# Sparse attention stage of a twelve-stage kernel: zero-padded keys, rotary terms read from PSUM, another order of its first projections

## The chip, the cores and the metric

The kernel runs on one core of a Trainium2 chip. Its engines are named as the profile names them: PE multiplies matrices (PEld is its weight load), DVE is the vector engine, ACT the scalar engine with its tables of functions, POOL the general engine, and SP issues the DMAs. The metric is the device time of one execution in microseconds (us); lower is better.

## The reference, cut to what matters

The program is two transformer blocks of depth 2, on 256 tokens of width 1024 in float32. The change is in the mixer of the first block's second layer, a sparse attention: 8 index heads score the keys, the 64 best causal keys of each query are kept, and 16 heads of 64 channels attend to these alone. Queries have 16 heads, while keys, values and index keys have one head that all share.

```python
q, k, v, qi, ki, wi = split_cols(h @ w_in, SA_SPLITS)        # 1024, 64, 64, 512, 64, 8 columns
q = apply_rope(rms_norm(q.reshape(b, L, ATT_HEADS, ATT_HEAD_DIM), q_norm), cos, sin)
k = apply_rope(rms_norm(k, k_norm)[:, :, None, :], cos, sin)[:, :, 0]
qi = apply_rope(qi.reshape(b, L, IDX_HEADS, IDX_DIM), cos, sin)
ki = apply_rope(ki[:, :, None, :], cos, sin)[:, :, 0]
...
logits = jnp.einsum('bthd,bsd->btsh', qib, ki).astype(jnp.float32)
score = jnp.einsum('btsh,bth->bts', jax.nn.relu(logits), wib.astype(jnp.float32)) * idx_scale
score = jnp.where(causal[None], score, -jnp.inf)
_, sel = lax.top_k(score, topk)                                # topk = 64
...
s = jnp.einsum('bthd,btkd->bthk', qb, k_sel).astype(jnp.float32) * att_scale
s = jnp.where(valid[:, :, None, :], s, -jnp.inf)
p = jax.nn.softmax(s, axis=-1).astype(v_sel.dtype)
return jnp.einsum('bthk,btkd->bthd', p, v_sel)                 # then @ w_out, added to x
```

## The kernel before, in words

Twelve stages follow one another: for each layer a feed-forward, a mixer and a feed-forward. The residual stays in two tiles of 128 tokens (`X[0]`, `X[1]`, the token tiles t0 and t1). Every large product is made of float32 split in two parts: `mm3` (L170 to L174) multiplies high by high (L172), low by high (L173) and high by low (L174) into one PSUM bank. Weights are made ready by `prep` (L105): SP fetches a unit into one of four `raw` tiles, ACT rounds it to the high part `wh` (L133) and DVE takes the difference as the low part `wl` (L137). For a few units `on_pool` (L142) puts the difference on POOL: those of the second half of the query projection and rows 3, 5 and 6 of the output projection `sa_w_out`. PSUM's eight banks are `pj` (3, projections), `pa` (3) and `pb` (2).

The order of the instructions on each engine isn't written out. A scheduler of the framework, which simulates the engines at build time, chooses it under priorities (`urgent` raises one) and pins (`after`: this comes behind that instruction). An engine works through its own list in order, so a late instruction holds up all behind it.

The sparse stage `sparse` (L896 to L1123) begins at about 788 us of the span. In the feed-forward before it the tables of the rotary terms (`rope_tables`) and rows 0 to 2 of `sa_w_out` are made ready. Then come, in program order:

- the projection of keys, values, index keys and index weights (200 columns, evacuated by `ev_kv`) and of the index queries (512 columns, `ev_qi`), each for both token tiles together (`proj_nat` goes through the k tiles and within one through both token tiles, then evacuates t0 and t1);
- `rope` (L904): on a copy of the projection in SBUF (ACT, L936, L955, L1012), POOL multiplies by the sine (`rt`, L907), DVE by the cosine (L908) and adds both (L909); PE transposes the result (`transp`, L918) and ACT copies it to SBUF (L920);
- `select(t)` (L971 to L1000): index scores of a pair of heads per bank (L980), where a head's product is 64 rows deep and lies in the upper or the lower half of the partitions; a ReLU on ACT (L983), the weighted sum of 8 heads on DVE (L987, L989), then eight rounds of `max` and `match_replace` (L995, L996) and the mask `mb[t]` (L997 to L1000);
- `proj_q(0)` and `proj_q(1)`, the queries of heads 0 to 7 and 8 to 15; the norm `qr` of each head goes into the scale of the exponential (L1019, L1021 on DVE, L1023 on POOL);
- the attention: `scores` fills a bank with four heads (t0, 128 keys) or two (t1, 256 keys), per head one product of depth 64 (L1043) and one that adds the mask (L1045, the mask as the moving operand of a unit matrix `idb`); DVE takes the maximum (L1048) and scales it (L1049); ACT takes the exponentials (L1052); `values` transposes them (L1059), copies them (L1063, L1065) and multiplies by `v` (L1070); `close` divides by the sums;
- the output projection, t0 and then t1 (from 908.32 us on), and the addition to `X` (L1110).

ACT holds one set of function tables at a time. `ex` (L962) is an exponential of a zero, pinned behind `ev_qi`'s copy, so that the load of the exponential's table comes there.

## Time and profile before

| what | value |
|---|---|
| time, median of 3 runs | 2453.47 us (2443.68, 2453.47, 2455.34) |
| span of the profiled execution, first to last instruction | 2446.0 us |
| PE busy | 2414.0 us, 99% |
| DVE, ACT, POOL busy | 1480.9, 1212.3, 183.1 us (61%, 50%, 7%) |
| granted clock of PE, mean | 0.987 |
| sparse stage up to its output projection | about 788 to 908 us |

The profiled execution has no time listed beside its span, and the time around the span isn't shown; the three runs lie from 2.3 us below the span to 9.3 us above it. Busy time is that of instructions that ran, so a PE at half clock counts as busy. The granted clock (PEclk) is a share of full speed, 1.00 for 2.4 GHz and 0.50 for 1.2 GHz. An idle time in brackets stands before the instruction that ended it, with what it waited for.

### The profile page before, as it was taken

How to read it: one execution, taken by the hardware profiler on the slowest of the kernel's cores; microseconds unless marked ns; L12 is line 12 of the kernel's file. 1: busy time of each engine (PE TensorE's matmuls, PEld its weight loads, DVE VectorE, ACT ScalarE, POOL GpSimd, SP SyncE). 2: the span in 40 equal slices, each digit the busy share in tenths (PEclk: the TensorE clock that was granted, in tenths of full speed). 3: DMA queues.
4: the chain of work that ended last, by engine and by line, in shares of the span. 5: the costliest groups of instructions: out<-in, count | busy, mean ns of one | idle time of the engine just before them, and what ended most of it. 6: DMA issues, size and time to landing. Idle time of an engine off the chain costs nothing.

```text
span 2446.0 us, 31525 instructions
## 1 busy us (share of the span) xinstructions
PE 2414.0 (99%) x11588; PEld 1979.5 (81%) x11588; DVE 1480.9 (61%) x2086; ACT 1212.3 (50%) x1868; POOL 183.1 (7%) x189
## 2 busy tenths in 40 slices
PE   8999999999999899999999999999999999999999
PEld 6888988888887678888888877888888887778887
DVE  5556786556555745556556685565565567756554
ACT  5445555445454435444445564454454455534543
POOL 0000330000000410000001020200000011101000
PEclk9999999999999879999999999999999999999999
DMA  7666545665665315655666543565566665335654
GB/s 237 192 193 181 146 126 177 199 186 177 205 214 159 114 35 163 189 186 189 189 188 188 163 129 110 171 209 188 181 198 189 190 184 160 117 104 172 202 186 136
DMA packets 301259, 417.15 MB, mean 171 GB/s; under 512 B 29168, under 2 KB 227248, under 8 KB 301104
## 3 DMA queue, kind: packets, MB, share of 16 engines
q1 hardware_dynamic: 300960, 414.66, 55.2%
q8 instruction: 91, 1.49, 0.3%
q14 instruction: 64, 0.52, 0.1%
q10 hardware_dynamic: 144, 0.48, 0.0%
HBM read 414.01 MB, written 1.05 MB: 170 GB/s over the span
## 4 chain that ended last, share of the span: by engine, by line
PE 95%; DVE 2%; issue 1%; DMA 1%; ACT 1%; POOL 0%; SPq 0%; DVEq 0%; POOLq 0%; ACTq 0%
PE pb L173 13%; PE pb L172 13%; PE pb L174 13%; PE pj L173 13%; PE pj L172 13%; PE pj L174 13%; PE pa L185 3%; PE pa L172 2%; PE pa L173 2%; PE pa L174 2%; PE pa L1043 1%; PE pa L809 1%; PE pa L1182 1%; DVE wl L137 1%; PE pb L1070 1%
## 5 line engine op out<-in xcount | busy, mean ns | idle before, releaser
L137 DVE TENSOR_TENSOR wl<-raw,wh 128x1024 fp32r<-128x1024 f32 x713 | 880.8, 1241 | 552.7 <-ACT wh L133 548.3
L133 ACT ACTIVATE wh<-raw 128x1024 fp32r<-128x1024 f32 (+1 forms) x720 | 755.5, 1054 | 579.2 <-PE pb L174 322.8
L172 PE MATMUL pb<-wh,qh 128*128 128x512 f32 x1408 | 551.6, 392 | 2.3 <-ACT qh L188 1.5
L173 PE MATMUL pb<-wl,qh 128*128 128x512 f32 x1408 | 550.1, 391 | 0.5 <-DVE wl L137 0.5
L174 PE MATMUL pb<-wh,ql 128*128 128x512 f32 x1408 | 549.8, 391 | 0.0
L172 PEld LDWEIGHTS pb<-wh,qh 128*128 128x128 f32 x1408 | 264.7, 188 | 58.3 <-ACT qh L188 1.8
L173 PEld LDWEIGHTS pb<-wl,qh 128*128 128x128 f32 x1408 | 264.8, 188 | 55.9 <-DVE wl L137 1.0
L174 PEld LDWEIGHTS pb<-wh,ql 128*128 128x128 f32 x1408 | 264.7, 188 | 55.6
L172 PE MATMUL pj<-wh,qh 128*128 128x512 f32 (+2 forms) x758 | 300.3, 399 | 1.9 <-ACT qh L188 1.7
L173 PE MATMUL pj<-wl,qh 128*128 128x512 f32 (+2 forms) x758 | 298.4, 394 | 1.3 <-DVE wl L137 1.3
L174 PE MATMUL pj<-wh,ql 128*128 128x512 f32 (+2 forms) x758 | 296.8, 395 | 0.3 <-DVE ql L189 0.3
L174 PE MATMUL pj<-wh,gl 128*128 128x512 f32 x432 | 173.8, 402 | 0.0
L172 PEld LDWEIGHTS pj<-wh,qh 128*128 128x128 f32 x758 | 143.7, 190 | 33.5 <-issue 3.9
L174 PEld LDWEIGHTS pj<-wh,ql 128*128 128x128 f32 x758 | 143.9, 190 | 32.2 <-issue 2.6
L173 PEld LDWEIGHTS pj<-wl,qh 128*128 128x128 f32 x758 | 144.0, 190 | 31.4 <-issue 2.9
L173 PE MATMUL pj<-wl,gh 128*128 128x512 f32 x432 | 168.5, 390 | 0.0
L172 PE MATMUL pj<-wh,gh 128*128 128x512 f32 x432 | 168.2, 391 | 0.0
L428 ACT ACTIVATE sg<-pb,nr 128x256 f32<-128x256 f32 x176 | 83.4, 474 | 148.3 <-PE pb L174 148.1
L430 DVE SCALAR_TENSOR_TENSOR g<-pb,nr,sg 128x256 f32<-128x256 f32 x176 | 84.6, 481 | 93.0 <-ACT sg L428 92.7
L188 ACT ACTIVATE gh<-pa 128x256 fp32r<-128x256 f32 x176 | 67.2, 382 | 130.9 <-PE pa L185 130.9
L257 POOL TENSOR_TENSOR nr<-nm,mhalf 128x1 f32<-128x1 f32 x24 | 14.2, 594 | 1471.9 <-DVE nm L255 1471.9
L189 DVE TENSOR_TENSOR gl<-pa,gh 128x256 fp32r<-128x256 f32 x176 | 74.4, 423 | 71.5 <-ACT gh L188 64.1
(522 smaller groups left out, 2908.2 us busy)
## 6 DMA issues: line engine op xcount, KB each, us to landing
raw<-in_ffn_w SPq DMA_DIRECT2D x352, 256.0 KB, 3.1
raw<-in_w_in SPq DMA_DIRECT2D x104, 512.0 KB, 4.0
raw<-in_ffn_w_gate SPq DMA_DIRECT2D x176, 256.0 KB, 2.9
raw<-in_ffn_w_up SPq DMA_DIRECT2D x176, 256.0 KB, 3.2
raw<-in_ffn_w_down SPq DMA_DIRECT2D x88, 512.0 KB, 3.6
raw<-in_ffn_w SPq DMA_DIRECT2D x88, 512.0 KB, 3.6
raw<-in_hy_w_in SPq DMA_DIRECT2D x44, 512.0 KB, 3.7
raw<-in_hy_w_out SPq DMA_DIRECT2D x16, 512.0 KB, 3.6
```

What stands on the lines that cost most here:

```text
L133: nc.scalar.activation(h[:, :n], r[:, :n], AF.Copy)
L137: eng.tensor_tensor(l[:, :n], r[:, :n], h[:, :n].bitcast(F32), op=OP.subtract)
L172: mm(out, a[0], b[0], start=start, stop=False)
L173: mm(out, a[0], b[1], start=False, stop=False)
L174: return mm(out, a[1], b[0], start=False, stop=stop)
L185: pe = nc.tensor.transpose(p[:, k * 128:(k + 1) * 128], src[:, k * 128:(k + 1) * 128], self.ident)
L188: act = nc.scalar.activation(hv, pv, AF.Copy)
L189: dve = nc.vector.tensor_tensor(lv, pv, hv.bitcast(F32), op=OP.subtract)
L428: nc.scalar.activation(sg, q[t][:, :256], AF.Silu, scale=rs[t])
L430: nc.vector.scalar_tensor_tensor(g, q[t][:, 256:], rs[t], sg, op0=OP.mult, op1=OP.mult)
L809: at["V", k] = nc.tensor.matmul(acc[t][:, h * dv:h * dv + dv], PT[:, j * 2 + b, :], vals(b, h), start=b == 0, stop=b == 1)
L1043: nc.tensor.matmul(S[:, j * nk:j * nk + nk].rearrange("p (t n) -> p t n", n=128), qT[b, t, g * 4 + h // 2, :], kkT[b, 0:t + 1, 1, :], star ...
```

## The change

- **Zero-padded keys.** The transposed keys lie in `kz` twice, once in the upper 64 partitions and once in the lower ones, with zeros in the other half. A product of depth 128 with the stacked queries of two heads then gives both heads' scores: 512 columns in one at t1, twice 256 at t0. This holds for the index scores and the attention's scores. `kz` is filled by two ACT copies of 64 partitions per tile and kind.
- **One mask product per bank.** The mask is the stationary or moving operand once for the 512 columns of a bank (`maskid` is -2^100 on the diagonal) and comes before the scores. The mask itself is one DVE instruction instead of two or three; the causal bias goes into the first step of the weighted sum (`cz`).
- **Rotary terms from PSUM.** `rope` reads the projection's bank and multiplies in place, all three instructions on DVE. The copy on ACT and POOL's product go away, and the bank is held until the third instruction. ACT's ReLU is in place in PSUM, and DVE's weighted sum reads PSUM.
- **Token tiles in turn.** `first_proj` multiplies keys and values of t0, index queries of t0, then both of t1, each evacuated at once.
- **First weights.** The first three units of `sa_w_in`, not rows 0 to 2 of `sa_w_out`, are made ready in the feed-forward before. Those rows' fetches and splits come in the sparse stage.
- **No pin on `ex`.** The exponential that loads the table has no pin any more.

```diff
+        maskid = C([128, 128], "mid", BF16)
+        nc.vector.tensor_scalar(maskid, ident, -BIG, None, op0=OP.mult)
+        cz, cm = C([128, 256], "cz"), C([128, 256], "cm")
...
+    def sa_in(self, j):
+        slot = (f"lh{j}", f"ll{j}") if j < 3 else None
+        if j < 2:
+            return self.unit(("sa_w_in", (0,), j * 4, 4, 1664, 72), ("sa_w_in", (0,), j * 4, 4, 1024, 128), slot=slot, pool="sa_out")
+        return self.unit(("sa_w_in", (0,), j * 2 - 4, 2, 1152, 512), slot=slot, pool="sa_out")
...
+        kz = T([128, 2, 2, 256], "kz")
+        nc.gpsimd.memset(kz[64:128, :, 0, :], 0.0)
+        nc.gpsimd.memset(kz[0:64, :, 1, :], 0.0)
...
-            nc.gpsimd.tensor_tensor(half(tmp), half(x)[:, :, ::-1, :], half(b.unsqueeze(1).to_broadcast([128, H, 64])), op=OP.mult)
-            nc.vector.tensor_tensor(out, x, a.unsqueeze(1).to_broadcast([128, H, 64]), op=OP.mult)
-            nc.vector.tensor_tensor(out, out, tmp, op=OP.add)
+            if r is None:
+                nc.vector.tensor_tensor(half(hv(tmp)), half(hv(x))[:, :, ::-1, :], half(wide(b)), op=OP.mult)
+                nc.vector.tensor_tensor(hv(x), hv(x), wide(a), op=OP.mult)
...
+            return nc.vector.tensor_tensor(out, two(x), two(tmp), op=OP.add)
...
+        def ev_qi(t, p):
+            o = T([128, 512], "qo", bufs=2)
+            rope(o.unsqueeze(1), p, cs2[:, t, :], sn2[:, t, :], 8)
             transp(qiT[:, t], o, 4, ("i", t))
             if t == 1:
-                with self.after(copied):
-                    nc.scalar.activation(self.small([128, 1], "ex"), self.zero[:, 0:1], AF.Exp)
+                nc.scalar.activation(self.small([128, 1], "ex"), self.zero[:, 0:1], AF.Exp)
...
+        def first_proj():
+            self.held()
+            us = [self.sa_in(j) for j in range(6)]
+            pin = None
+            for t in range(2):
+                for n, (mine, step, w, ev) in enumerate(((us[:2], 4, 200, ev_kv), (us[2:], 2, 512, ev_qi))):
+                    p = self.pj()
+                    with self.after(pin):
+                        for k in range(8):
+                            h, l = mine[k // step]
+                            last = self.mm3(p[:, :w], self.kt(hT, k, t), (h[:, k % step, :], l[:, k % step, :]), k == 0, k == 7)
+                    pin = last
+                    with self.urgent():
+                        ev(t, p)
+            self.hold = None
...
+            for h0 in range(0, 8, hn):
                 q = self.pa()
+                for j in range(0, hn, 2):
+                    at["x", t, h0] = nc.tensor.matmul(q[:, j * nk:j * nk + 2 * nk].rearrange("p (d n) -> p d n", d=2),
+                                                      qiT[:, t, (h0 + j) // 2, :], kz[:, 0, :, 0:nk], start=True, stop=True)
+                nc.scalar.activation(q, q, AF.Relu)
+                for j in range(hn):
+                    nc.vector.scalar_tensor_tensor(sc, q[:, j * nk:j * nk + nk], wi[:, t, h0 + j:h0 + j + 1],
+                                                   cz[:, 256 - nk:] if h0 + j == 0 else sc, op0=OP.mult, op1=OP.add)
...
+            at["mb", t] = nc.vector.scalar_tensor_tensor(mb[t], sc, -3.2e38, cm[:, 256 - nk:], op0=OP.is_gt, op1=OP.subtract)
...
             def ev_q(t, p):
-                x = T([128, 1024 - 512 * t], ("lh7", "lhx")[t])[:, :512]
-                nc.scalar.activation(x, p, AF.Copy)
...
+                sq = T([128, 512], "on")
+                nc.scalar.activation(sq, p, AF.Square)
+                o = T([128, 512], "qo", bufs=2)
+                rope(o.unsqueeze(1), p, qa[:, t, :], qb[:, t, :], 8)
...
-            for j, h in enumerate(hs):
-                nc.tensor.matmul(S[:, j * nk:j * nk + nk].rearrange("p (t n) -> p t n", n=128), qT[b, t, g * 4 + h // 2, :], kkT[b, 0:t + 1, 1, :],
-                                 start=True, stop=False)
-                nc.tensor.matmul(S[:, j * nk:j * nk + nk], identb, mb[t], start=False, stop=True)
+            nc.tensor.matmul(Sv, maskid, mb[t].unsqueeze(1).to_broadcast([128, hn, nk]), start=True, stop=False)
+            for j in range(0, hn, 2):
+                nc.tensor.matmul(Sv[:, j:j + 2, :], qT[:, t, g * 4 + (h0 + j) // 2, :], kz[:, 1, :, 0:nk], start=False, stop=j + 2 == hn)
...
-                self.early = {b: lambda u=u: self.sa_w_out(u) for u, b in enumerate((5, 6, 7))}
+                self.early = {b: lambda u=u: self.sa_in(u) for u, b in enumerate((5, 6, 7))}
```

The scheduler moves instructions in three places of which the prediction speaks. In the rows an instruction stands with its line, then what it writes, an arrow and what it reads, by the program's names with numbers. Lines are those of the kernel they are taken from.

PE around the index queries' transposes, before: `ll_1535` and `llx` are the rotated index queries of t0 and t1, `pj_7506` the third bank of the queries.

```order
L172 MATMUL pj_7391<-wh_7190,qh_6938 128x512
L173 MATMUL pj_7391<-wl_7191,qh_6938 128x512
L174 MATMUL pj_7391<-wh_7190,ql_6939 128x512
L172 MATMUL pj_7506<-wh_7412,qh_6938 128x512
L918 MATMUL pb_7249<-const_81,ll_1535_7244 128x128 x4
L918 MATMUL pb_7262<-const_81,llx_7257 128x128 x4
L980 MATMUL pa_7273<-kkT_7050,qiT_7049 128x128 x2
```

And now, where `pj_7218` is the index queries' product of t1 and `qo_7156` the rotated index queries of t0:

```order
L172 MATMUL pj_7218<-wh_6986,qh_6948 128x512
L173 MATMUL pj_7218<-wl_6987,qh_6948 128x512
L946 MATMUL pb_7161<-const_81,qo_7156 128x128 x4
L174 MATMUL pj_7218<-wh_6986,ql_6949 128x512
L172 MATMUL pj_7218<-wh_6986,qh_6948 128x512
L173 MATMUL pj_7218<-wl_6987,qh_6948 128x512
L174 MATMUL pj_7218<-wh_6986,ql_6949 128x512
```

The transposes of t0 have moved into the product of t1, and those of t1 (`qo_7243`) stand 40 rows on, between products of the queries.

ACT at the first exponentials, now (`on` are the squares of the queries, `sE` the exponentials; before, the table load stood at L962, behind `ev_qi`'s copy and ahead of the index scores):

```order
L1025 ACTIVATE on_7536<-pj_7462 128x512
L1025 ACTIVATE on_7555<-pj_7463 128x512
L1058 ACT_TABLE_LOAD
L1058 ACTIVATE sE_7582,rs_7574<-pa_7575,snm_7579,qr_1584_7441 128x128
L950 ACTIVATE qT_7061<-pb_7543 128x512
L1058 ACTIVATE sE_7582,rs_7574<-pa_7575,snm_7579,qr_1584_7441 128x128 x3
```

The load has moved to the first exponential itself; the exponential `ex` (L978) stands at the start of the program.

DVE behind the second mask, now (`mb_1497` is the mask of t1, `ll` and `wl` low parts of the output projection's weights, `snm` the maxima of a bank of scores):

```order
L1016 MATCH_REPLACE sc_1548_7298<-m_1560_7340,sc_1548_7298 128x256
L1017 SCALAR_TENSOR_TENSOR mb_1497_7063<-sc_1548_7298,cm_6023 128x256
L137 TENSOR_TENSOR ll_1599_7485<-raw_7482,lh_1598_7484 128x1024
L137 TENSOR_TENSOR ll_1602_7503<-raw_7500,lh_1601_7502 128x1024
L137 TENSOR_TENSOR ll_1605_7521<-raw_7518,lh_1604_7520 128x1024
L137 TENSOR_TENSOR wl_7891<-raw_7888,wh_7890 128x1024
L1054 TENSOR_REDUCE snm_7628<-pa_7624 128x4
```

The three `ll` splits are new in this stage and stand ahead of the last maximum of t0. Elsewhere the order is the same but for the start of the first feed-forward, which takes 17 small DVE instructions of the tables, and the first of the two mixers of the second block, where the scheduler puts some 600 rows of PE into another order.

## Rows read from the trace of the kernel before

**Rows 1.** The page: engines' share of the span, then the chain that ended last
```profile
PE 2414.0 (99%) x11588; PEld 1979.5 (81%) x11588; DVE 1480.9 (61%) x2086; ACT 1212.3 (50%) x1868; POOL 183.1 (7%) x189
...
PE 95%; DVE 2%; issue 1%; DMA 1%; ACT 1%; POOL 0%; SPq 0%; DVEq 0%; POOLq 0%; ACTq 0%
```

**Rows 2.** Busy time by stretch of the sparse stage: from:to, length, engines, PEclk, DMA share, GB/s
```profile
812.00:831.00 19.00, 13.57 (x49) 9.54 (x48) 11.55 (x19) 4.11 (x9) 6.37 (x3) 0.64 0.27 84
831.00:848.00 17.00, 17.00 (x74) 12.93 (x71) 15.78 (x32) 6.97 (x10) 9.91 (x5) 1.00 0.26 70
848.00:888.00 40.00, 36.35 (x129) 25.45 (x127) 27.34 (x61) 20.21 (x56) 14.83 (x8) 0.53 0.19 63
```

**Rows 3.** Timeline of PE: start, us, engine, line, operation, count, [idle before <-releaser]
```profile
816.31 0.98 PE L918 MATMUL pb<-const,ll 128*128 128x128 f32 x4 [3.49 <-DVE ll L909]
819.06 1.08 PE L918 MATMUL pb<-const,llx 128*128 128x128 f32 x4 [1.77 <-DVE llx L909]
...
829.66 0.59 PE L174 MATMUL pj<-wh,ql 128*128 128x512 f32 x1
...
851.57 1.11 PE L918 MATMUL pb<-const,ll 128*128 128x128 f32 x4 [2.96 <-DVE ll L909]
...
864.36 0.79 PE L1043 MATMUL pa<-kkT,qT 64*128 64x128 f32 x2 [0.69 <-ACT qT L920]
...
908.32 0.48 PE L172 MATMUL pj<-lh,qh 128*128 128x512 f32 x1
908.63 0.39 PE L173 MATMUL pj<-ll,qh 128*128 128x512 f32 x1
908.87 0.40 PE L174 MATMUL pj<-lh,ql 128*128 128x512 f32 x1
```

**Rows 4.** Timeline of PE: two heads' scores at half clock, then two at full clock
```profile
855.18 0.79 PE L1043 MATMUL pa<-kkT,qT 64*128 64x128 f32 x2
...
856.12 0.79 PE L1043 MATMUL pa<-kkT,qT 64*128 64x128 f32 x2
...
888.23 0.70 PE L1043 MATMUL pa<-kkT,qT 64*128 64x256 f32 x2
888.86 0.28 PE L1045 MATMUL pa<-mb,idb 128*128 128x256 bf16 x1
889.07 0.70 PE L1043 MATMUL pa<-kkT,qT 64*128 64x256 f32 x2
```

**Rows 5.** Timeline of PE: score products of the later latent attention, 128 and 64 rows deep
```profile
1471.40 0.70 PE L1425 MATMUL pa<-mk,mq 128*128 128x256 f32 x2
1472.03 0.70 PE L1426 MATMUL pa<-mk,mq 64*128 64x256 f32 x2
```

**Rows 6.** Timeline of PE: index scores of the second token tile, two banks, then one
```profile
830.18 1.14 PE L980 MATMUL pa<-kkT,qiT 64*128 64x256 f32 x8
...
832.38 1.13 PE L980 MATMUL pa<-kkT,qiT 64*128 64x256 f32 x4
```

**Rows 7.** Timeline of DVE: rope, a mask's first step, and a maximum that reads PSUM
```profile
813.34 2.83 DVE L909 TENSOR_TENSOR ll<-ll,rt 128x512 f32<-128x512 f32 x1
...
850.84 0.68 DVE L909 TENSOR_TENSOR ll<-ll,rt 128x512 f32<-128x512 f32 x1
...
862.54 1.85 DVE L997 TENSOR_SCALAR sc<-sc 128x256 f32<-128x256 f32 x1
864.31 0.68 DVE L1048 TENSOR_REDUCE snm<-pa 128x4 f32<-128x512 f32 x1
```

**Rows 8.** Timeline of POOL: weight splits, two at a time
```profile
812.83 5.54 POOL L137 TENSOR_TENSOR wl<-raw,wh 128x1024 fp32r<-128x1024 f32 x2
...
861.89 4.70 POOL L137 TENSOR_TENSOR wl<-raw,wh 128x1024 fp32r<-128x1024 f32 x2
```

**Rows 9.** Timeline of ACT: the table of the exponential
```profile
809.82 1.28 ACT L962 ACT_TABLE_LOAD   x1
```

**Rows 10.** The page, groups: weight splits on DVE
```profile
L137 DVE TENSOR_TENSOR wl<-raw,wh 128x1024 fp32r<-128x1024 f32 x713 | 880.8, 1241 | 552.7 <-ACT wh L133 548.3
```

More of the change, by code (lines that the diff above doesn't have):

```diff
@@ L951, in sparse @@
-        self.proj_nat(hT, 8, "sa_w_in", (0,), [(1664, 72), (1024, 128)], urgent(ev_kv))
+            o = T([128, 2, 128], "ko", bufs=2)
+            ov = o.rearrange("p i (d n) -> p i d n", d=2)
+            for i in range(2):
+                if i == 0:
+                    rope(ov[:, 0], p[:, 0:64], cs2[:, t, :], sn2[:, t, :], 1, 2)
+                    nc.scalar.activation(wi[:, t, :], p[:, 64:72], AF.Copy, scale=8.0 ** -0.5 * 64.0 ** -0.5)
+                    nc.scalar.activation(v[:, t, :], p[:, 136:200], AF.Copy)
+                else:
+                    rope(ov[:, 1], p[:, 72:136], ka[:, t, :], kb[:, t, :], 1, 2, r)
+                q = transp(None, o[:, i, :], 1, ("k", i, t))
+                for d in range(2):
+                    b = slice(d * 64, d * 64 + 64)
+                    nc.scalar.activation(kz[b, i, d, ts], q[b, 0:128], AF.Copy)
@@ L968, in sparse @@
         mb = [T([128, 128 * (t + 1)], f"mb{t}", BF16) for t in range(2)]
[L969 removed]
         def select(t):
             nk = 128 * (t + 1)
[L973 removed]
+            hn = 4 // (t + 1)
             sc = T([128, nk], f"sc{t}")
[L975 removed]
+            for h0 in range(0, 8, hn):
                 q = self.pa()
[L977 to L992 removed]
@@ L1023, in ev_q @@
                 nc.gpsimd.tensor_tensor(qr[t, j], m, self.mhalf[:, :8], op=OP.pow)
-            if j == 0:
-                self.feed = [None, at["x", 0, 3], at["x", 1, 0]]
             self.proj_nat(hT, 8, "sa_w_in", (0,), [(j * 512, 512)], ev_q)
@@ L1077, in close @@
             self.to_T(on, t, yq[g])
+        first_proj()
+        with self.urgent():
+            select(0)
+            select(1)
         proj_q(0)
@@ L1082, in sparse @@
         proj_q(1)
-        banks = [(t, g, a + b) for t, g in ((0, 0), (0, 1), (1, 0), (1, 1)) for a in range(0, 8, 8 // (t + 1)) for b in range(2)]
+        banks = [(t, g, h0) for t, g in ((0, 0), (0, 1), (1, 0), (1, 1)) for h0 in range(0, 8, 4 // (t + 1))]
         Es = {}
```

98 lines of the change are left out of this document (27 added, 71 removed).

## The prediction

> **What bounds the kernel now.** First the page: PE is busy for 2414.0 of 2446.0 us, and 95% of the chain that ended last is PE [rows 1]. Only PE's idle time, work that it need not do, and time at half clock can be won. So the next view is busy time by stretch, with the granted clock [rows 2]. In the sparse stage it stands at 0.64 in 812 to 831 us, at 1.00 until 848, at 0.53 until 888; the mean over the span is 0.987, so there is little to win elsewhere. DVE is busy for 15.78 of the 17.00 us before 848: it sets when the masks are ready. Third, PE's timeline says what ended each idle time [rows 3]: 3.49 and 1.77 us before the transposes of the index queries, 2.96 and 0.69 us around those of the queries, always behind DVE's rope or the copy after it. The clock falls behind the first and the third of these waits.
>
> How long it stays down is read from the durations: from 816.3 to 829.9 us [rows 3], and from 851.6 to 887.9, since the first head at full clock begins at 888.23 [rows 4]. These are 13.6 us with 1.8 idle, and 36.3 us with 0.7 idle. At half clock half of PE's busy time is lost: 5.9 and 17.8 us. With the waits (3.49 + 1.77 + 2.96 + 0.69 = 8.9 us) 32.6 us lie open, nearly all between 812 and 908.32 us, where the output projection begins [rows 3].
>
> **The change part by part**, against the span of 2446.0 us.
>
> *First projections in turn, rope on DVE.* The 48 products of t1's index queries now stand behind t0's projection, and t0's rope runs beside them. t1's rope and transposes are 40 rows later, among the queries' products. The waits of 3.49 and 1.77 us go: -5.25. Something is late instead: the low part of t1's normed input stands on DVE behind three rope instructions of t0. One such instruction takes 0.68 us beside an idle POOL [rows 7]; I put back 0.85 us, little more than one. Sum **-4.4**. No wait there should keep the clock up: **-5.9**.
>
> In front of PE stands DVE, so its price matters. Of the old rope, an add of two SBUF operands took 2.83 us at 813.34 us, while POOL split weights (812.83 us, 5.54 us for two), and 0.68 us at 850.84 [rows 7, 8]. A maximum that read PSUM began at 864.31 us, inside POOL's split of 861.89 (4.70 us for two), and took 0.68 us all the same, where a mask step on SBUF took 1.85 [rows 7, 8]. So reading PSUM takes rope out of POOL's way, and POOL has no rope left. There are now 18 rope instructions of 512 columns (six evacuations of three), at 0.68 us 12.2 us. I take 0.68; the other end is 2.83. Against this speaks the Trainium skill, VectorE: DVE Perf Modes, Rules for kernel authors: for many operations on a matmul's output it advises to copy it to SBUF first. By that rule each in-place product would cost more than from SBUF; the two readings at 0.68 us show no such difference, and the sum goes by them.
>
> *Query products and the last ropes.* The 2.96 and 0.69 us waits go: -3.65. But the order now puts the last two query ropes with no projection left to cover them. Three rope instructions, a reduction and a mask round lie ahead on DVE, some 4 x 0.68 = 2.7 us, less what the first banks cover; I take a wait of 2.6. The table of the exponential now loads at the first score: 1.28 us [rows 9], with the exponential itself behind it; I take 1.8 us. Before, that load was beside other work, so this is a cost of the lost pin. Behind the second mask DVE splits three rows of output weights and a fourth unit, 4 x 1.24 = 5.0 us [rows 10], with the last maximum of t0 queued behind them; some 3.3 us of this are covered by t0's values and the first t1 scores, which leaves 1.7. New waits 2.6 + 1.8 + 1.7 = 6.1: sum **+2.5**. The bounds are 0 (the first banks hide them all) and 10. With these rows three fetches of 512 KB move behind the query weights on SP's queue, where the DMA engines were busy for 0.19 to 0.27 of the time [rows 2], and three copies move to ACT, busy for 20 of 40 us. Their `raw` tiles come free when POOL has split the weights of the second query half, so a copy on ACT can wait for POOL and hold up the last ReLU of t1 behind it: that is in the bound of 10, and it would come in again through the second mask.
>
> *The clock in the attention.* With waits of 2 us and more close together I expect it to fall again near the first scores. Scores now start about 12 to 15 us earlier than 855.18 us, and denser work follows. In the first stretch, dense from 820 us on, it had come back by 829.9, 13.6 us after it fell; behind the wait of 2.96 it took 36.3 us. I take 14 us, the nearer row for dense work: 7 us lost in place of 17.8, **-10.8**. Bounds: 0 lost, or half clock to the end of the attention.
>
> *Score products.* A t1 head costs 0.84 us at full clock, from 888.23 to 889.07, 0.63 for the product and 0.21 for the mask [rows 4]; a bank of two 1.68. Now a bank has one mask product of 512 columns (0.25 us, an estimate from the 0.28 of 256 columns and the 0.24 us from start to start of two projection products of 512 [rows 3, 4]) and one product of 512 columns, 128 deep. The nearest row is a pair of 256 columns, 0.63 us at depth 128 and 0.63 at depth 64 [rows 5]: depth costs nothing. Twice that is 1.25 and, with one weight load saved, I take 1.1. A bank is 1.35, eight save 2.6 us. A t0 head took 0.94 us at half clock [rows 4], so a bank of four 1.9 at full; now 0.25 and two products of 256 columns, 1.4: four save 2.1. Together -4.7 (bounds -2 and -6).
>
> The index scores go the other way. Eight records (four heads) took 1.14 us and four (two heads) 1.13 [rows 6]: where two banks on different halves of the partitions follow each other, they overlap. Padded products fill all 128 rows and can't. t1 had three such groups, the last like the second, 3.3 us; four products of 1.1 make +1.1. t0 ran at half clock, so its price is less plain; with half the columns I add 0.7. Sum of scores **-2.9**. The Trainium skill, TensorEngine Tiling (Array Packing), Key Properties, says that tiles of 64 rows work independently, and so speaks against padding; had the two heads of an old t1 bank overlapped, it would have cost 0.63 + 2 x 0.21 = 1.05 us, and padding would lose 0.3 us a bank instead of winning 0.33. In the attention the mask over all 128 rows stands between the heads, and at 0.84 us a head the rows show no overlap.
>
> *The rest.* The 17 small instructions at the start may delay the first feed-forward, and the reordered mixer may lose or win a little; PE was at 99% there: **+0.5** (bounds -1 and +5).
>
> Sum: -4.4 - 5.9 + 2.5 - 10.8 - 2.9 + 0.5 = **-21.0 us**, span 2425.0 us. The span lies 7.5 us below the median of the runs, 2453.47; I take the difference over to the median, 2432.5: **2432 us**.
>
> **The rivals.**
> A, *half clock to the end.* The forecast's new waits hold the clock down over the whole attention. For: behind a wait of 2.96 us it took 36.3 us. Some 28 us of full-clock work would then take 56 instead of 28 + 7: 21 us more, about 2453 us. Against: the work is denser, and the waits before 812 us go.
> B, *no fall.* Banks of t0 cover the ropes, the clock stays up: -7 more, and perhaps half of the 6.1 us of waits: 2422 to 2425, with all of them gone 2419. For: DVE is freed of POOL's stretching, so the masks come earlier. Against: the table load has no cover.
> C, *DVE stretched.* If the 18 ropes cost what the adds at 813 us cost, 18 x 2.15 = 39 us of DVE time fall between the first projections and the second mask, which the forecast has at some 851 us. Slower by over 0.5% needs 33 us, 15 of 18 stretched: 2432 + 39 = 2471 us. By the Trainium skill, SBUF — State Buffer, Summary: rules for kernel authors, two SBUF inputs on DVE and a POOL operation that reads SBUF block each other; here one input of each rope is in PSUM, and the row at 864.31 us speaks against C.
> D, *given back elsewhere.* The reordered mixer or the start lose 10 us: 2442 us. Nothing in the rows shows it, as PE waits hardly anywhere.
>
> **How the numbers follow.** Under 0.5% (12.3 us) a measurement of this kernel can't tell a difference: its own three runs spread over 11.7 us. Forecast 0.52 (2424 to 2441), A 0.16, B 0.17, C 0.07, D 0.08. Faster by over 0.5% (below 2441.2) are the forecast, B and a third of D: 0.72. Within 0.5%: A and the rest of D, 0.21. Slower: 0.07. The range takes B from 2414 (with the bounds of the scores) to most of A at 2450.
>
> **What would show it.** The windows: clock 1.00 in 812 to 838, 20 us or more taken off the time up to the output projection (now 908.32). PE's waits: none on `ll`, `llx`; up to 3 us each on the last `qo` and on `sE`, behind a table load. Half clock for about 14 us in the attention: over 30 means A, none means B. DVE: rope at 0.68 us; near 2.8 means C. Score banks of 1.35 us at full clock; 1.7 would make the padding worth nothing. Wrong would be an output projection that begins at 908 us or later, or waits of 5 us and more outside the stage.

## The result, and the profile after the change

The changed kernel takes 2421.36 us (median of four runs, 2419.86 to 2424.27) against 2453.55 us before (four runs beside it); the ratio is 0.9882 with a 95% interval of 0.9856 to 0.9908. The forecast was 2432 us in a range of 2414 to 2450, faster. The profiled execution took 2419.86 us, 1.8 us more than its span of 2418.1; that span is 27.9 us shorter than before's, where the working had 21.0. The runs of before that stood beside the experiments had medians of 2447.97, 2444.46 and 2445.07 us, so the first few lay high. Each run below is therefore set against its own runs of before by a ratio; runs of the changed forms, whose times spread less, are also compared by their times.

The page has the same picture as [rows 1]: PE bounds the kernel, and 28.6 us of its busy time are gone.

```profile
PE 2385.4 (99%) x11520; PEld 1962.5 (81%) x11520; DVE 1474.7 (61%) x2084; ACT 1208.4 (50%) x1868; POOL 173.9 (7%) x183
...
PE 96%; DVE 2%; DMA 1%; ACT 1%; POOL 0%; issue 0%; SPq 0%; POOLq 0%; ACTq 0%; DVEq 0%
```

Busy time by stretch answers [rows 2] (length, busy time of PE, PEld, DVE, ACT and POOL with counts, then PEclk, DMA share, GB/s):

```profile
812.00:831.00 19.00, 19.00 (x84) 14.53 (x82) 15.03 (x45) 10.81 (x16) 11.13 (x6) 1.00 0.38 116
831.00:848.00 17.00, 10.24 (x43) 7.38 (x42) 14.11 (x37) 6.44 (x14) 4.70 (x3) 0.82 0.11 31
848.00:888.00 40.00, 36.58 (x196) 29.24 (x195) 27.12 (x50) 23.58 (x71) 4.67 (x2) 0.82 0.29 93
```

The first fall of the clock is gone (0.64 before, 1.00 now), the second is shallower (0.53, now 0.82). But between 831 and 848 us PE was never idle before and now lacks 6.76 us. PE's timeline, the answer to [rows 3 and 4], says where:

```profile
836.17 0.39 PE L1050 MATMUL pa<-mb,mid 128*128 128x512 bf16 x1
...
837.26 0.38 PE L1050 MATMUL pa<-mb,mid 128*128 128x512 bf16 x1
...
844.00 1.12 PE L946 MATMUL pb<-const,qo 128*128 128x128 f32 x4 [5.28 <-DVE qo L941]
846.59 0.48 PE L1065 MATMUL pj<-const,sE 128*128 128x128 f32 x1 [1.47 <-ACT sE L1058]
...
858.94 3.60 PE L1076 MATMUL pb<-v,sPT 128*128 128x64 f32 x16 [2.52 <-ACT sPT L1069]
865.02 1.12 PE L185 MATMUL pa<-const,on 128*128 128x128 f32 x4 [0.90 <-DVE on L1082]
...
870.13 0.38 PE L1050 MATMUL pa<-mb,mid 128*128 128x512 bf16 x1
...
871.21 0.38 PE L1065 MATMUL pj<-const,sE 128*128 128x128 f32 x2
...
884.26 0.48 PE L172 MATMUL pj<-lh,qh 128*128 128x512 f32 x1
```

No transpose of the index queries waits any more. In their place stand waits of 5.28, 1.47, 2.52 and 0.90 us. A bank of t0 costs 1.09 us (836.17 to 837.26), one of t1 1.08 (870.13 to 871.21). The output projection begins at 884.26 instead of 908.32 us.

The trace's record of the clock, set beside PE's rows, parts the stage (from the normed input's transposes, 786.49 us, to the first product of the feed-forward behind it, 909.39 us; before from 787.75 to 933.44). Half of PE's busy time inside a stretch of half clock counts as lost, the rest as work at full clock:

| us | before | after | difference |
|---|---|---|---|
| length | 145.7 | 122.9 | -22.8 |
| PE idle | 11.1 | 11.6 | +0.5 |
| lost at half clock | 23.9 | 8.0 | -15.9 |
| work at full clock | 110.7 | 103.3 | -7.4 |
| of it score products with masks | 19.7 | 13.1 | -6.6 |

The half-clock stretches were 13.7 and 37.5 us before; now they are 842.0 to 852.2 and 859.0 to 869.3, 10.2 us each. The other 5.1 us of the span's 27.9 lie outside the stage: before's profiled execution was at half clock for 10.2 us from 2103 us on, about 5 us lost, and the changed one wasn't. No part of the change acts there.

What stands behind the wait of 5.28 us? First ACT and POOL:

```profile
834.43 1.06 ACT L133 ACTIVATE wh<-raw 128x1024 fp32r<-128x1024 f32 x1 [5.43 <-DMA raw<-in_sa_w_out]
835.39 0.58 ACT L1009 ACTIVATE pa<-pa 128x512 f32<-128x512 f32 x1
...
844.69 1.28 ACT L1058 ACT_TABLE_LOAD   x1 [3.81 <-DVE snm L1055]
```

```profile
828.37 2.40 POOL L137 TENSOR_TENSOR wl<-raw,wh 128x1024 fp32r<-128x1024 f32 x1 [3.69 <-PE pb L946]
```

Then DVE:

```profile
836.01 1.00 DVE L1011 SCALAR_TENSOR_TENSOR sc<-pa,wi,sc 128x256 f32<-128x256 f32 x2 [2.47 <-ACT pa L1009]
...
843.26 0.68 DVE L941 TENSOR_TENSOR qo<-pj,rt 128x512 f32<-128x512 f32 x1
...
852.29 0.43 DVE L1017 SCALAR_TENSOR_TENSOR mb<-sc,cm 128x256 bf16<-128x256 f32 x1
852.63 3.49 DVE L137 TENSOR_TENSOR ll<-raw,lh 128x1024 fp32r<-128x1024 f32 x3
856.03 1.22 DVE L137 TENSOR_TENSOR wl<-raw,wh 128x1024 fp32r<-128x1024 f32 x1
857.17 0.68 DVE L1054 TENSOR_REDUCE snm<-pa 128x4 f32<-128x512 f32 x1
```

ACT stood 5.43 us before the copy of an output row whose `raw` tile came free only when POOL's split of 828.37 us ended (the trace has its fetch issued at 830.79 us and landed at 834.32). The last ReLU of t1 is queued behind that copy; DVE idles for 2.47 us on it, and t0's rope of the second query half, done at 843.94, is queued behind t1's weighted sum. This wait on `qo` is called the wait on the last rope below. The late ReLU is some 2.5 us of it; the rest is DVE's: from 836.01 to 843.94 us DVE is busy without a break, and mask rounds, reductions and a rope step of t1 stand between the three steps of that rope.

The other wait, 2.52 us on the transposed probabilities (`sPT`), ended with ACT:

```profile
857.35 1.06 ACT L133 ACTIVATE wh<-raw 128x1024 fp32r<-128x1024 f32 x1 [4.07 <-DMA raw<-in_sa_w_out]
858.31 0.58 ACT L1069 ACTIVATE sPT<-pj 128x512 f32<-128x512 f32 x1
```

The four splits (4.7 us) behind the second mask stand in front of it, as the prediction had them, but by the same path as the first wait: the first of them ends at 853.85 us and frees a `raw` tile, the fetch into it is issued at 853.87 and lands at 857.32, and the copy of the probabilities is queued on ACT behind the copy of that row.

### The profile page after: what moved, and what is told of

It reads as the page before. It is cut to its first block, busy times and chain, and to the rows that moved or that the text cites. A ratio compares the mean times of both kernels' runs of the same rounds, so it can differ in the third digit from the quotient of the medians.

```text
span 2418.1 us, 31362 instructions
## 1 busy us (share of the span) xinstructions
PE 2385.4 (99%) x11520; PEld 1962.5 (81%) x11520; DVE 1474.7 (61%) x2084; ACT 1208.4 (50%) x1868; POOL 173.9 (7%) x183
## 3 DMA queue, kind: packets, MB, share of 16 engines
q8 instruction: 90, 1.47, 0.2%
## 4 chain that ended last, share of the span: by engine, by line
PE 96%; DVE 2%; DMA 1%; ACT 1%; POOL 0%; issue 0%; SPq 0%; POOLq 0%; ACTq 0%; DVEq 0%
PE pj L172 13%; PE pj L174 13%; PE pb L173 13%; PE pb L172 13%; PE pb L174 13%; PE pj L173 13%; PE pa L185 3%; PE pa L173 2%; PE pa L172 2%; PE pa L174 2%; PE pa L809 1%; PE pa L1192 1%; PE pa L797 0%; DVE wl L137 0%; PE pa L1436 0%
## 5 line engine op out<-in xcount | busy, mean ns | idle before, releaser
L133 ACT ACTIVATE wh<-raw 128x1024 fp32r<-128x1024 f32 x717 | 753.2, 1055 | 579.2 <-PE pb L174 322.8
L172 PE MATMUL pj<-wh,qh 128*128 128x512 f32 (+1 forms) x738 | 292.5, 399 | 0.7 <-ACT qh L188 0.7
L173 PE MATMUL pj<-wl,qh 128*128 128x512 f32 (+1 forms) x738 | 290.4, 393 | 1.2 <-DVE wl L137 1.2
L174 PE MATMUL pj<-wh,ql 128*128 128x512 f32 (+1 forms) x738 | 288.6, 395 | 0.0
L174 PEld LDWEIGHTS pj<-wh,ql 128*128 128x128 f32 x738 | 138.6, 188 | 32.1 <-issue 3.1
L172 PEld LDWEIGHTS pj<-wh,qh 128*128 128x128 f32 x738 | 138.5, 188 | 32.0 <-issue 4.3
L173 PEld LDWEIGHTS pj<-wl,qh 128*128 128x128 f32 x738 | 138.8, 188 | 29.4 <-DVE wl L137 2.0
L257 POOL TENSOR_TENSOR nr<-nm,mhalf 128x1 f32<-128x1 f32 x24 | 14.1, 589 | 1450.0 <-DVE nm L255 1450.0
```

What stands on the lines that cost most here:

```text
L133: nc.scalar.activation(h[:, :n], r[:, :n], AF.Copy)
L172: mm(out, a[0], b[0], start=start, stop=False)
L173: mm(out, a[0], b[1], start=False, stop=False)
L174: return mm(out, a[1], b[0], start=False, stop=stop)
```

## The experiments

All twelve in one table; idle, lost and work are parted as above, over the same stage, in each run's own profile.

| run | time (us) | ratio to before [95%] | idle | lost | work |
|---|---|---|---|---|---|
| s_old | 2447.15 (10 runs) | 0.9992 [0.9973, 1.0011] | 6.8 | 30.5 | 109.5 |
| s_padmask | 2419.85 (1) | | 11.5 | 6.8 | 104.2 |
| s_64 | 2441.46 (1) | | 7.6 | 27.4 | 105.5 |
| s_256 | 2424.29 (1) | | 11.9 | 8.3 | 103.4 |
| b_pad | 2430.67 | 0.9938 [0.9918, 0.9958] | 16.4 | 10.5 | 105.2 |
| proj_old | 2415.44 | 0.9873 [0.9851, 0.9896] | 7.6 | 1.7 | 104.6 |
| noturn | 2417.52 | 0.9885 [0.9863, 0.9906] | 10.2 | 6.1 | 104.2 |
| rope_proj | 2414.55 | 0.9868 [0.9849, 0.9887] | 7.1 | 3.4 | 105.6 |
| relu_ex | 2418.66 | 0.9888 [0.9868, 0.9908] | 8.4 | 6.7 | 103.5 |
| spread | 2412.80 | 0.9860 [0.9840, 0.9881] | 5.1 | 3.2 | 103.3 |
| b1_spread_turn | 2412.32 | 0.9855 [0.9832, 0.9878] | 6.0 | 0.0 | 105.2 |
| b2_old_turn | 2418.80 | 0.9884 [0.9867, 0.9901] | 8.1 | 3.3 | 105.7 |

**What the padding is worth.** Four forms of the score products stand in the changed kernel. `s_old` takes each head alone again, 64 rows deep, with its own mask product; the heads of a bank have one parity, as before.

```diff
-            nc.tensor.matmul(Sv, maskid, mb[t].unsqueeze(1).to_broadcast([128, hn, nk]), start=True, stop=False)
-            for j in range(0, hn, 2):
-                nc.tensor.matmul(Sv[:, j:j + 2, :], qT[:, t, g * 4 + (h0 + j) // 2, :], kz[:, 1, :, 0:nk], start=False, stop=j + 2 == hn)
+            for j in range(hn):
+                nc.tensor.matmul(Sv[:, j, :], qT[b, t, g * 4 + h0 // 2 + j, :], kz[b, 1, d, 0:nk], start=True, stop=False)
+                nc.tensor.matmul(Sv[:, j, :], maskid, mb[t], start=False, stop=True)
```

> The changed kernel with the scores of the kernel before: per head one product of depth 64 and one mask product, heads of one parity in a bank; all else as changed. Both theories expect a t1 head at 0.84 us of full clock again and about 8 us more of PE work than the changed kernel in the attention (19.7 against 11.9 us), so a time some 6 to 14 us above the changed kernel, with the clock's part open.

Measured: no difference from before. All the rest of the change together, without padded keys in the attention's scores (the index scores stay padded), gives nothing. PE idles 4.3 us less than before and has 1.2 us less work, but 6.6 us more are lost at half clock. To the changed kernel this is 26 us, far more than the 6 to 14 expected, and 22.5 of the difference is clock: half clock from 843.6 to 908.4 us, 64.9 us on end. So the next run changes depth alone: the same instructions in the same form, but over all 128 rows against the padded keys.

```diff
-                nc.tensor.matmul(Sv[:, j, :], qT[b, t, g * 4 + h0 // 2 + j, :], kz[b, 1, d, 0:nk], start=True, stop=False)
+                nc.tensor.matmul(Sv[:, j, :], qT[:, t, g * 4 + h0 // 2 + j, :], kz[:, 1, d, 0:nk], start=True, stop=False)
```

> As s_old, with the same instructions in the same order, but the products read the zero-padded keys and are 128 rows deep. Theory S (a change between products of 64 and of 128 rows costs PE about 0.15 us each time): a t1 head falls from 0.84 to 0.54 us, 0.43 for the product and 0.11 for the mask. Theory L (what counts is how many products there are and how long each is; 256 columns cost 0.63 us): a head stays at 0.84 us.

Busy time by stretch of `s_old`, then of `s_padmask`:

```profile
842.00:862.00 20.00, 15.95 (x53) 10.02 (x52) 17.19 (x40) 9.63 (x30) 5.15 (x3) 0.54 0.25 91
862.00:882.00 20.00, 18.66 (x66) 13.35 (x66) 7.28 (x13) 8.78 (x25) 2.81 (x2) 0.50 0.30 94
882.00:902.00 20.00, 20.00 (x67) 12.60 (x65) 4.94 (x12) 6.39 (x19) 0.00 (x0) 0.50 0.00 1
```

```profile
842.00:862.00 20.00, 13.88 (x80) 12.16 (x81) 18.56 (x39) 12.60 (x35) 5.47 (x4) 0.76 0.31 107
862.00:882.00 20.00, 18.84 (x122) 16.03 (x121) 12.49 (x25) 12.94 (x42) 1.04 (x1) 0.82 0.25 79
882.00:902.00 20.00, 20.00 (x111) 17.21 (x111) 5.99 (x12) 3.53 (x9) 0.56 (x1) 1.00 0.00 1
```

PE's 612 records of the stage stand in the same order in both. In the first 40 us PE lacks 5.4 us in `s_old` and 7.3 in `s_padmask`, so the denser one is the one whose clock stays down: 0.50 against 0.82, then 0.50 against 1.00, with PE busy for all of the last 20 us in both. The 128-deep form has stretches of 6.8 and 10.2 us and takes 27 us less, in a single run; the ten runs of `s_old` lie within 4.7 us, all with a mean clock of 0.984 to 0.987, where `s_padmask` has 0.996 and the changed kernel's runs 0.994 to 0.996. Its score work is also shorter, 14.1 against 19.6 us. On PE's timeline a head at full clock with its mask takes 0.58 us from start to start in `s_old`:

```profile
837.39 0.48 PE L1053 MATMUL pa<-kz,qT 64*128 64x128 f32 x2
837.80 0.23 PE L1054 MATMUL pa<-mb,mid 128*128 128x128 bf16 x1
837.97 0.48 PE L1053 MATMUL pa<-kz,qT 64*128 64x128 f32 x2
```

and 0.33 us in `s_padmask`:

```profile
836.69 0.44 PE L1052 MATMUL pa<-kz,qT 128*128 128x128 f32 x2
836.96 0.22 PE L1053 MATMUL pa<-mb,mid 128*128 128x128 bf16 x1
837.02 0.44 PE L1052 MATMUL pa<-kz,qT 128*128 128x128 f32 x2
```

The head in `s_old` has two changes of depth more, so one costs 0.12 us. At half clock the same two heads take 0.95 and 0.64 us, 0.15 for a change: its price hardly follows the clock, so the column "lost" is somewhat too high for the 64-deep forms, and "work" too low.

`s_64` and `s_256` do the same with one mask product per bank: heads of 64 rows, then of 128 rows, 256 columns at t1.

> One mask product of 512 columns per bank, then per head a product of 64 rows. Theory S: two changes of depth in a bank, a t1 bank 0.22 + 2 x 0.43 + 2 x 0.15 = 1.38 us. Theory L: 0.22 + 2 x 0.63 = 1.48 us, and the same as s_256.

> As s_64 with the same instructions in the same order, but the products of single heads are 128 rows deep (padded keys). Theory S: no change of depth, a t1 bank 0.22 + 2 x 0.43 = 1.08 us, as in the changed kernel with one product of 512 columns. Theory L: 1.48 us, since two products of 256 columns stand in place of one of 512.

The clock follows depth again, with PE's products in the same order in both: half clock for 58.0 us at 64 rows, twice 10.2 us at 128 (both have 6.8 us more far behind the stage). `s_64` has 24 changes of depth where `s_old` has 64, and is held down nearly as long, so the number of changes is not what decides. A t0 bank at full clock takes 1.40 us from mask to mask in `s_64`:

```profile
837.36 0.39 PE L1052 MATMUL pa<-mb,mid 128*128 128x512 bf16 x1
...
838.76 0.39 PE L1052 MATMUL pa<-mb,mid 128*128 128x512 bf16 x1
```

and 1.10 us in `s_256`:

```profile
838.18 0.38 PE L1051 MATMUL pa<-mb,mid 128*128 128x512 bf16 x1
...
839.28 0.38 PE L1051 MATMUL pa<-mb,mid 128*128 128x512 bf16 x1
```

That is 0.15 us for each of two changes, while products of one depth behind each other take the same 0.11 us in both. So theory S holds: a t1 head of `s_padmask` takes 0.54 us at full clock and a t1 bank of `s_256` 1.08, where theory L had 0.84 and 1.48. Beside this, what else the change does to the scores is small: one mask per bank takes 0.9 us of score work (14.1 to 13.2), two heads in one product 0.1 (13.2 to 13.1), and neither shows in the times.

`b_pad` goes the other way: before, with nothing but the 128-deep padded scores.

```diff
-                nc.tensor.matmul(S[:, j * nk:j * nk + nk].rearrange("p (t n) -> p t n", n=128), qT[b, t, g * 4 + h // 2, :], kkT[b, 0:t + 1, 1, :],
+                nc.tensor.matmul(S[:, j * nk:j * nk + nk], qT[:, t, g * 4 + h // 2, :], kz[:, h % 2, 0:nk],
```

> The kernel before with one edit: the scores' products read zero-padded keys and are 128 rows deep, a mask product per head as before. Theory C (the gain is PE's clock: products of 64 rows hold it at half, those of 128 let it come back): the long stretch at half clock, 37.5 us before, shortens to 7 to 14 us, scores cost about 14.3 us of full clock in place of 19.7, and the time is 2425 to 2432 us. Theory D (the gain needs the denser order of the other parts): the stretch stays over 25 us and the time is above 2438 us.

Measured: 2430.67 us, about half of what the change gives, and theory C's time. PE's products stand in the order of before. The old waits stay (3.44 and 2.08 us before the index queries' transposes), and so does the first half-clock stretch of 13.7 us; the second shrinks from 37.5 to 6.8 and 3.4 us. So the rest of the change is worth some 9 us where the scores are padded, and nothing where they aren't (`s_old`).

**What the first projections are worth.** `proj_old` takes both token tiles together again and makes rows 0 to 2 of the output weights ready in the feed-forward before.

```diff
-        first_proj()
+        self.proj_nat(hT, 8, "sa_w_in", (0,), [(1664, 72), (1024, 128)], urgent(ev_kv))
+        self.proj_nat(hT, 8, "sa_w_in", (0,), [(1152, 512)], urgent(ev_qi))
...
-                self.early = {b: lambda u=u: self.sa_in(u) for u, b in enumerate((5, 6, 7))}
+                self.early = {b: lambda u=u: self.sa_w_out(u) for u, b in enumerate((5, 6, 7))}
```

> The changed kernel with the first projections as before (both token tiles together, index queries after keys and values; rows 0 to 2 of the output weights made ready early). Prediction's step: the waits of 3.5 and 1.8 us on the index queries' rope come back, less what rope from PSUM saves, and the clock falls there for 13.6 us: 8 to 11 us slower than the changed kernel, about 2430 us. Rival: rope on DVE alone had removed those waits, and the time is within 3 us of the changed kernel.

Measured: 2415.44 us (2414.70 to 2415.59), about 6 us less than the change's 2421.36 (2419.86 to 2424.27). The times don't overlap; the ratios, with the spread of before in them, do. Neither old wait is back, the wait on the last rope is 2.49 us instead of 5.28, and in the stage one half-clock stretch of 3.4 us is left. PE's timeline of it:

```profile
842.97 0.66 PE L946 MATMUL pb<-const,qo 128*128 128x128 f32 x4 [2.49 <-DVE qo L941]
...
846.18 1.21 PE L1065 MATMUL pj<-const,sE 128*128 128x128 f32 x3 [0.73 <-ACT sE L1058]
```

`noturn` undoes only the turn and leaves the rows where the change has them.

```diff
-            for t in range(2):
-                for n, (mine, step, w, ev) in enumerate(((us[:2], 4, 200, ev_kv), (us[2:], 2, 512, ev_qi))):
-                    p = self.pj()
+            for mine, step, w, ev in ((us[:2], 4, 200, ev_kv), (us[2:], 2, 512, ev_qi)):
+                p = [self.pj(), self.pj()]
```

> The changed kernel with one thing undone: the first projections run both token tiles together again, but start as soon as their first rows are there, and every row of the projection weight stays behind the scores, as in the change. This parts the two things that the run with the old first projections undid at once (2415.44 us against 2421.36). Theory E, the moved weight rows cost: about 2421 us (2418 to 2424), the waits of 5.28 us on the query's last rope and 1.47 us on the exponentials are still there within 1 us, and so is a half-clock stretch of about 10 us there. Theory T, running the token tiles in turn costs: about 2415 us (2413 to 2418), the wait on the last rope under 2 us, and at most one stretch of half clock.

Measured: 2417.52 us (2416.13 to 2423.39), between the two. The wait on the last rope is 2.82 us, that on the exponentials 1.93, with two half-clock stretches of 6.8 us. The time is theory T's, the waits and stretches are neither's; neither expectation holds alone, and the intervals of all three kernels overlap: how the 6 us divide between turn and rows stays open.

`rope_proj` is `proj_old` with the ropes of the queries and index queries in the old form (copy on ACT, sine product on POOL, two steps on DVE from SBUF).

```diff
+            if r is None and H == 8:
+                xs = T([128, 512], "xq", bufs=2)
+                nc.scalar.activation(xs, x, AF.Copy)
+                nc.gpsimd.tensor_tensor(half(hv(tmp)), half(hv(xs))[:, :, ::-1, :], half(wide(b)), op=OP.mult)
```

> The kernel with the old first projections (2415.44 us, waits of 0.62 and 0.58 us in them, one half-clock stretch of 3.4 us), in which the ropes of the query and key projections go the old way again: ScalarE copies the bank, GpSimd multiplies by the sine table, VectorE works from SBUF. Theory R, the rope from PSUM took the waits of 3.49 and 1.77 us in the first projections away, and with them the first fall of the clock: waits of some 3 and 1.5 us there come back, and a half-clock stretch of 10 to 14 us beginning near 800 to 816 us; 2422 to 2430 us. Rival, the rope's place does not matter because these ropes are hidden either way: within 3 us of 2415.4, and no new stretch of half clock ahead of the first score.

The rival holds: 2414.55 us. The price of a rope is as the prediction had it, 0.68 us from PSUM against up to 2.88 from SBUF beside POOL's split, here on DVE and POOL:

```profile
810.91 2.88 DVE L939 TENSOR_TENSOR qo<-qo,rt 128x512 f32<-128x512 f32 x1
```

```profile
810.40 2.84 POOL L137 TENSOR_TENSOR wl<-raw,wh 128x1024 fp32r<-128x1024 f32 x1
```

But PE has products to do meanwhile, and the transposes wait for nothing:

```profile
814.03 0.60 PE L952 MATMUL pb<-const,qo 128*128 128x128 f32 x4
817.00 0.60 PE L952 MATMUL pb<-const,qo 128*128 128x128 f32 x4
```

Two things differ from before. Before, 109 projection products (PE's records from the normed input's transposes on) stood ahead of the index queries' transposes of both token tiles; in `rope_proj` it is 124 for t0 and 135 for t1. That is 15 and 26 products of 0.23 us more, 3.4 and 5.9 us, about as much as the old waits together. And DVE ends its two adds at 814.39 us (810.91 + 3.48 for both), where before PE waited for the second until 819.06 [rows 3], in a stage that now starts 1.3 us earlier. Both come from the order that the scheduler found for the rest of the change; no run undid that order alone.

**What the moved rows cost, and what helps.** `relu_ex` holds the late ACT copy behind the last ReLU, and `ex` behind its copy as it was before.

```diff
+              with self.after(copied):
                 nc.scalar.activation(self.small([128, 1], "ex"), self.zero[:, 0:1], AF.Exp)
...
+                at["relu"] = nc.scalar.activation(q, q, AF.Relu)
...
+        self.copy_pins = [None, at["relu"]]
```

> The changed kernel with two pins: the weight copy of row 4 comes behind the last ReLU on ACT, and the exponential that loads the table behind the index queries' last copy. Theory Q (the last ReLU stood 5.4 us behind a weight fetch and made DVE late): PE's wait on qo falls from 5.3 to 2 or 3 us, that on sE from 1.5 to about 0.3, and if the clock then doesn't fall at 841 us another 3 us come back: 2413 to 2417 us. Rival: DVE has too much to do there anyway, the wait on qo stays above 4.5 us, the time within 2 us of the changed kernel.

Measured: 2418.66 us. The wait on the last rope falls to 3.04 us and the 1.47 us on the first exponentials to 0.19, so both causes were as read. But 2.96 us turn up on exponentials at 858.46 us, and two stretches of 6.8 us stay. 3.5 us are won on these two waits, the time is 2.7 us less, and the intervals overlap; theory Q's 2413 to 2417 us is missed.

`spread` pins `ex`, gives rows 0 to 2 to POOL (and 3, 5 and 6 to DVE), and prepares rows 3 to 7 one by one behind the banks of scores, instead of four in a row behind the second mask.

```diff
-        return name == "sa_w_in" and c0 == 512 or name == "sa_w_out" and k0 in (3, 5, 6)
+        return name == "sa_w_in" and c0 == 512 or name == "sa_w_out" and k0 in (0, 1, 2)
...
+                if not self.dry and 4 <= i < 9:
+                    self.prep_pin, self.copy_pins = at["nm"], [at["E"]] if True else ()
+                    self.prep()
```

> The changed kernel with the table's pin, rows 0 to 2 of the output weights split on POOL, and rows 3 to 7 prepared one by one behind the banks of scores, so that no block of four splits stands on DVE behind the second mask. Theory W (that block and the weight copies on ACT cause PE's waits of 2.5 and 0.9 us at 859 to 865 us and the second fall of the clock): both waits under 0.7 us, no second stretch at half clock, 2408 to 2414 us. Rival: POOL's splits stretch DVE's operations on SBUF, the masks come later, and the time is above 2419 us.

Measured: 2412.80 us (2408.98 to 2413.45), with the token tiles still in turn and the rows still late. Theory W holds: its two waits are 0.38 us and none, and no second stretch at half clock is left. How much of it is the pin and how much the rows was not parted. Between 848 and 888 us PE lacks 0.38 us instead of 3.42:

```profile
831.00:848.00 17.00, 14.10 (x58) 10.27 (x57) 16.40 (x47) 7.07 (x23) 4.51 (x3) 0.85 0.07 25
848.00:888.00 40.00, 39.62 (x239) 32.22 (x238) 24.33 (x46) 23.33 (x67) 0.00 (x0) 0.98 0.22 67
```

Last, the wait on the last rope itself: `b1_spread_turn` and `b2_old_turn` run the second half of the query projection in turn too, on `spread` and on `proj_old` with `ex` pinned.

```diff
-            self.proj_nat(hT, 8, "sa_w_in", (0,), [(j * 512, 512)], ev_q)
+            self.proj_nat(hT, 8, "sa_w_in", (0,), [(j * 512, 512)], ev_q, first=j == 1)
```

> The best kernel so far (split of rows 0 to 2 on GpSimd, rows 3 to 7 one by one behind the banks: 2412.8 us), with the second half of the query projection too running its token tiles in turn, so that the last rope of tile 0 is worked out while tile 1 is still being multiplied. Theory: what is left of the wait on the query's last rope there (2.24 us and the others, 0.9 and 0.4) shrinks to under 1 us, the half-clock stretch of 6.8 us behind it (3.1 us lost) goes, and the time is 2406 to 2411 us. Rival: VectorE is the one that is late, the wait moves to the next transpose or to the exponentials at the same size, and the time is 2411 to 2415 us.

> The kernel with the old first projections and rows 0 to 2 split early (2415.44 us), with the second half of the query projection in turn, and the index's exponentials held behind its copy. Its wait of 2.49 us on the query's last rope is the longest that is left in the stage. Theory: that wait shrinks to under 1 us and the 3.4-us stretch of half clock goes (1.7 us lost): 2410 to 2414 us. Rival: the same idle time turns up behind the exponentials or the transposes of the probabilities: 2414 to 2418 us.

In both the wait on the rope is gone and stands at the exponentials, and in the second also at the first mask. PE's waits, first of `b1_spread_turn`, then of `b2_old_turn`:

```profile
844.88 0.77 PE L1065 MATMUL pj<-const,sE 128*128 128x128 f32 x2 [2.88 <-ACT sE L1058]
```

```profile
840.35 0.39 PE L1050 MATMUL pa<-mb,mid 128*128 128x512 bf16 x1 [1.62 <-DVE mb L1017]
845.70 0.77 PE L1065 MATMUL pj<-const,sE 128*128 128x128 f32 x2 [1.94 <-ACT sE L1058]
```

The rivals were right on the place: 2412.32 us can't be told from `spread`'s 2412.80, and 2418.80 us is 3 us behind `proj_old`, above even the rival's range. In `b1_spread_turn` the clock doesn't fall in the stage at all, and the stage isn't shorter for it than `spread`'s by more than 0.4 us (111.2 against 111.5): it has 0.9 us more idle time and 1.9 us more work. DVE is busy for 16.51 of the 17 us before 848 us there: it can do its work in another order, but has no room to be early everywhere.

## Why the prediction was right, and where it was not

The sign and the range held, and the mechanism (waits, then a clock that falls behind them and a cheaper score bank) is where the time came from. Within the stage the sum was near, -21.5 (the -21.0 without the +0.5 for the rest) against -22.8, because errors of both signs cancelled; that it came so near is luck.

- **Clock in the attention (-10.8) and in the first projections (-5.9).** Together -16.7 forecast, -15.9 measured: the first fall gave back its 5.9 us, the attention 9.9. The step "denser work follows" failed as a cause: of `s_old` and `s_padmask` the denser one kept the clock down for 64.9 us, the other for 17.1 in two pieces. What the runs put in its place is the depth of the products. Rival A, half clock to the end, is what the change would have met without padding the attention's scores: 2447 us.
- **Score products (-4.7).** Measured -6.6: a bank costs 1.08 us at both token tiles, where 1.35 was forecast for t1. (For t0 the text gives 0.25 and 1.4; four banks of 1.65 would save 1.0 us, not the 2.1 in the sum, which goes with a bank of 1.4.) The step that failed is "depth costs nothing". The rows that it took [rows 5] alternate between the depths:

```profile
1470.78 0.70 PE L1426 MATMUL pa<-mk,mq 64*128 64x256 f32 x2
...
1472.66 0.70 PE L1425 MATMUL pa<-mk,mq 128*128 128x256 f32 x2
```

  So products of both depths pay a change there, 0.63 us from start to start. Behind and ahead of products of its own depth the 128-deep one takes 0.43 us, as in `b_pad`:

```profile
872.37 0.60 PE L1052 MATMUL pa<-kz,qT 128*128 128x256 f32 x2
872.80 0.27 PE L1054 MATMUL pa<-mb,idb 128*128 128x256 bf16 x1
```

  Depth by itself costs nothing, but a change of it does, and padding takes the changes away.
- **Index scores (+1.8).** About 0. The step that failed is "four products of 1.1". A padded product of 512 columns takes 0.86 us:

```profile
830.52 1.02 PE L1007 MATMUL pa<-kz,qiT 128*128 128x512 f32 x2
830.97 0.80 PE L173 MATMUL pj<-wl,qh 128*128 128x512 f32 x1
831.61 0.40 PE L174 MATMUL pj<-wh,ql 128*128 128x512 f32 x1
```

  From 830.52 to 831.61, less 0.23 for the projection product between, are 0.86 us, four of them 3.4, where the three overlapping groups of before took 3.3 [rows 6]. t0's take 1.7 us, where before's took 3.2 at half clock, 1.6 by half.
- **First projections in turn (-4.4).** The waits of 3.49 and 1.77 us did go. The step "t0's rope runs beside them" is not why: they stay away without the turn and with the old rope (`proj_old`, `rope_proj`), where the counts show more products ahead on PE and DVE done earlier. What was put back, 0.85 us for the low part of t1's normed input, was right: 0.89 us. In the form the change has, turn and moved rows cost some 6 us.
- **New waits (+6.1).** The places were right, the price too low: 5.28, 1.47, 2.52 and 0.90 us, 10.2 in all, at the upper bound of 10 that was given. The path of that bound is what happened: an ACT copy waits for a `raw` tile that POOL frees late, and holds up the last ReLU of t1. The 2.52 us came by it too, with a tile that DVE frees late; the prediction had only DVE's queue there. With 3.65 us of old waits gone the sum was +6.5 instead of +2.5.
- **The rest (+0.5).** The start and the reordered mixer give nothing that can be seen; what the start wins (1.3 us less up to the stage) is lost behind it. 5 us of the span's difference came from before's own profiled execution, whose half-clock stretch near 2103 us no term had.
- **Rivals.** C, DVE stretched, is refuted: the rope at 808.57, 809.28 and 810.02 us takes 0.68, 0.70 and 0.69 us beside a POOL split of 2.39 us that begins at 808.99. B, no fall, needs another order of the weight splits and came out in `b1_spread_turn`. D did not show.

## What to carry to other kernels

Where PE's clock falls and doesn't come back although PE is busy, look at the shape of the products in that stretch before looking for waits: here zero rows that do no useful work bought 27 us in the rewritten kernel and 14 us in the one before, and pairs of runs that changed depth alone showed it. A gain that follows from a whole rewrite should be undone part by part: here the parts don't add up. The padding alone gave about half, the other parts alone nothing, and together they gave more than both; 8.6 us more lay in spreading the weight splits, with the table's pin. A wait moved to another place on a full engine (DVE here) isn't won.

## What the runs showed of the hardware that was not expected

- **Depth and the clock.** With products 64 rows deep the granted clock stayed at the lower of its two levels (1.2 GHz) for 64.9, 58.0 and, before, 37.5 us; with the same products 128 rows deep, in the same order on PE, it came back to 2.4 GHz after 3.4 to 10.2 us. The 64-deep heads don't bring it down by themselves: `s_old`'s first eight ran at 2.4 GHz (837.39 to 841.9 us), and so did before's behind 888.23 us [rows 4], after 3.9 us of other products. Nor is it enough to leave them out: in `s_old` none ran from 863.9 to 874.8 us, with 1.3 us of idle time in it, and the clock stayed down. What decides it stays open.
- **A change of depth costs PE 0.12 to 0.20 us.** Per change it is 0.12 (`s_old` against `s_padmask`), 0.15 (`s_64` against `s_256`), 0.15 (a t1 head of 0.84 us before, 0.54 in `b_pad`) and 0.20 ([rows 5], 0.63 against 0.43). The Trainium skill, TensorEngine Tiling (Array Packing), Key Properties, says that a change of tiling mode drains the engine; these rows agree, and give the price.
- **PSUM keeps DVE out of POOL's way.** The same rope step took 2.88 us from SBUF beside a POOL split and 0.68 from PSUM. The Trainium skill, SBUF — State Buffer, Summary: rules for kernel authors, says that two SBUF inputs on DVE and a POOL operation that reads SBUF block each other; the row agrees.
- **Before's spread is clock.** Its runs from 2442.0 to 2459.58 us go with mean clocks from 0.991 down to 0.982; the changed kernel's runs spread over 4.4 us.
